# A three-layer float32 block on one core: the depthwise conv's VectorE sums kept in PSUM, its steps spread wider, and SBUF pools padded to multiples of 512 bytes

## The chip, the cores and the metric

One core of a Trainium2 chip. The time is microseconds (us) of device time of one launch; the profile is one execution of the same program. TensorE multiplies out of SBUF into PSUM (8 banks of 512 float32 per partition), VectorE, ScalarE and GpSimd work on SBUF, VectorE and ScalarE on PSUM too, and SyncE issues the DMAs.

## What is computed

Three layers over 512 tokens of width 1024, all float32. The first layer is differential attention, a gated FFN with a width-3 conv, and a gated embedding; the second has windowed attention in place of the first. The third, which the change touches, mixes a conv branch and an attention branch, and ends in an FFN without a conv:

```python
proj = h @ w_in                      # 1024 conv columns, q, k, v, forget, two gates of 1024
a = a_in[..., :512] * sigmoid(a_in[..., 512:])
a = causal_depthwise_conv(a, w_dw, b_dw)          # 512 channels, 31 taps
y_conv = silu(layernorm(a, g_ln, b_ln)) @ w_conv_out
y_attn = forgetting_attention(q, k, v, f) @ w_attn_out
merged = sigmoid(gate_a) * y_conv + sigmoid(gate_b) * y_attn
x = x + merged @ w_out
x = x + (silu(g) * u) @ w_ffn_out    # g, u = rmsnorm(x) @ w_ffn_in
```

## The kernel before

Activations lie with channels on the partitions and the 512 tokens along the free axis. A float32 product is made of three float32r ones: each operand is split into a high part and a rest, and `mm3` (L185) issues high*high (L187), high*rest (L188) and rest*high (L189). Weights come in units of 128x1024 by a DMA on SyncE's queue, ScalarE casts the high part `wh` (L156), VectorE subtracts for the rest `wl` (L157); two raw and three split units are in flight. `dense` (L292) makes one 128x512 output of 24 matmuls. The stationary operand is the weight, the moving one the activation: `xO`, `xV` and `xq` from the pool `xp`, `gh` and `gl` (the FFN's hidden tiles) from the pool `gp`, `mg` (half of the merged branch in the third layer) from a pool `mg`.

In `mix` (L857) the third layer's first half is built. The depthwise conv is done off TensorE: four chunks of 128 channels, 31 taps each. `glu` and `glu_gate` leave a chunk's input in `pads[m]` and `accs[m]` takes the sum. Chunks 2 and 3, and the last 11 taps of chunk 1, belong to GpSimd: a product into a scratch tile (`tap`, three buffers) on GpSimd itself during the attention heads (L915) or on ScalarE afterwards (L917), and an add on GpSimd (L918). All 31 taps of chunk 0 and the first 20 of chunk 1 are VectorE's: L909 for the first tap of a chunk, then `scalar_tensor_tensor` with the sum read and written in place (L911). `keep` holds the order of these as written. During the eight heads a few GpSimd taps follow each step (`TAPS`). Then come 16 gates (`gate`, L1074: one `dense` each, evacuated by L1076 into `tb` or `ga`, then Tanh), 8 products of the attention branch (`attn_conv(tb[m], 1, ox)`, 12 matmuls each, moving operand `xq`), 8 of the conv branch (`attn_conv(t, 0, cx)`, moving operands `cxh` and `cxl`), and `w_out2`.

`conv_step(i)` is called after gate i. For the first `CSTEP` gates it issues an even share of the taps that are left, afterwards one step of `conv_norm` (L1095), the layer norm over the four chunks: sum over chunks (L1090 to L1092), split, two matmuls against ones (`ps_cs`), centring (L1104) and squares, sum, mean by matmul (L226), inverse root, a broadcast matmul (`ps_bc`), scaling (L1116), SiLU and split into `cx`.

The order on an engine is not the order of the code alone: a list scheduler at build time takes what is ready on its own estimated timeline, earlier code first. A matmul output takes the next PSUM bank of a cycle (`WIDE`, six banks; outside wide stretches two): `acc` has two, `sc` three, `po` one; `tp`, two more, is for transposes and small sums. In the wide stretch of the gates the heads' `po` bank is part of the cycle.

SBUF is laid out pool after pool, each tile rounded up to 32 bytes, the first one (`sp`) at 128 bytes past a multiple of 512. Added up so, every large tile of the pools `hp`, `wp`, `xp` and `fp` (`h`, `wr`, `wh`, `wl`, `xq`, `xO`, `xV`, scratch) starts 32 bytes past a multiple of 512, and those of the pools opened after `sm` (`gh`, `gl`, `mg`, `rt`, `kst`, `tb`) start 192 bytes past one. A weight block inside a unit is 512 bytes wide, so it keeps its unit's offset.

Of the kernel before, what the change touches and what calls it, by code (L numbers as in the profile page):

```python
# [11 lines left out]
F32 = mybir.dt.float32  # L12
F32R = mybir.dt.float32r
I32 = mybir.dt.int32
AF = mybir.ActivationFunctionType
ALU = mybir.AluOpType
# [3 lines left out]
P = 128  # L20
D = 1024
T = 512
KD = D // P
# [24 lines left out]

VT = (31, 20)
TAPS = ((0, 1),) * 5 + ((0, 2),) * 3  # L50
CSTEP = 7

BANKS = {"acc": 2, "sc": 3, "po": 1}
WIDE = ("acc", "sc", "acc", "sc", "sc", "po")
# [5 lines left out]
_SPW = 0  # L60
# [24 lines left out]
_CNW = 641  # L85
# [6 lines left out]
def build(tc, nc, a, out):  # L92
    c = Ctx()
    es = ExitStack()
    cp = es.enter_context(tc.tile_pool(name="cp", bufs=1))
# [4 lines left out]
    sm = es.enter_context(tc.tile_pool(name="sm", bufs=4))  # L100
    dr = es.enter_context(tc.tile_pool(name="dr", bufs=1, space=bass.MemoryType.DRAM))
    acc = es.enter_context(tc.tile_pool(name="acc", bufs=2, space=PSUM))
    att = es.enter_context(tc.tile_pool(name="att", bufs=2, space=PSUM))

    V, S, G, TE, Q = nc.vector, nc.scalar, nc.gpsimd, nc.tensor, nc.sync


    sp = cp.tile([P, _SPW], F32, name="sp")
    cn = cp.tile([P, 641], F32, name="cn")
    onesf = cp.tile([P, P], F32, name="onesf")  # L110
    onesr = cp.tile([P, P], F32R, name="onesr")
    epsc = cp.tile([P, 1], F32, name="epsc")
    Q.dma_start(out=sp[:, 0:KD], in_=a["sp"][:, 0:KD])
    V.memset(onesf, 1.0)
    V.memset(epsc, EPS)
# [6 lines left out]
    def spc(name, i=0, n=1):  # L122
        o, w = _SP[name]
        return sp[:, o + i : o + i + n]

    def rd(t):
        return t.bitcast(F32)
# [49 lines left out]
    def split(hi, lo, src, scale=None):  # L177
        if scale is None:
            S.copy(out=hi, in_=src)
            V.tensor_tensor(out=lo, in0=src, in1=rd(hi), op=ALU.subtract)  # L180
        else:
            S.activation(out=hi, in_=src, func=AF.Copy, scale=scale)
            V.scalar_tensor_tensor(out=lo, in0=src, scalar=scale, in1=rd(hi), op0=ALU.mult, op1=ALU.subtract)  # L183
# [19 lines left out]
    def row_mm(ps, rt, eng, stop):  # L203

        r2 = sm.tile([P, 2, 4], F32R, tag="r2", name="r2")
        V.tensor_copy(r2[:, 0], rt)
        V.tensor_tensor(out=r2[:, 1], in0=rt, in1=rd(r2[:, 0]), op=ALU.subtract)
        for z in range(2):
            dg = fp.tile([P, 4, P], F32R, tag="C", name="dg")
            eng.tensor_tensor(  # L210
                out=dg,
                in0=ident[:, None, :].to_broadcast([P, 4, P]),
                in1=rd(r2[:, z])[:, :, None].to_broadcast([P, 4, P]),
                op=ALU.mult,
            )
            TE.matmul(ps, onesr, dg.rearrange("p a b -> p (a b)"), start=z == 0, stop=z == 1 and stop)
# [6 lines left out]
    def token_mean(ss, dst, scale, eps=EPS):  # L223
        ps = att.tile([P, 4], F32, tag="tp", name="ps_tm")
        for t in range(4):
            TE.matmul(ps[:, t : t + 1], ss[:, t * P : (t + 1) * P], onesf[:, 0:1], start=True, stop=True)  # L226
        V.tensor_scalar(out=dst, in0=ps, scalar1=scale, scalar2=eps, op0=ALU.mult, op1=ALU.add)
# [52 lines left out]
    tags = {"next": cycle(("acc",))}  # L280

    def wide(on):

        tags["next"] = cycle(WIDE if on else ("acc",))

    def bank(shape=(P, T)):
        t = next(tags["next"])
        return (acc if t == "acc" else att).tile(list(shape), F32, tag=t, name="ps_d", bufs=BANKS[t])
# [139 lines left out]
    def diff_attention(nm, nxt):  # L428
        x = nm.x
        pes = ExitStack()  # L430
        ap = pes.enter_context(tc.tile_pool(name="ap0", bufs=2, reuse_waits="tile"))
        lam = sm.tile([P, 1], F32, tag="lam", name="lam", bufs=1)
        lt = sm.tile([P, 2, 64], F32, tag="lt", name="lt", bufs=1)
        lv = spc("lam", 0, 256).rearrange("p (a b d) -> p a b d", a=2, b=2)
        V.tensor_tensor(out=lt, in0=lv[:, :, 0], in1=lv[:, :, 1], op=ALU.mult)
# [421 lines left out]
    def mix(nm, nxt):  # L857
# [4 lines left out]
        ma = aes.enter_context(tc.tile_pool(name="ma", bufs=1, reuse_waits="tile"))  # L862
        trir = ma.tile([P, P], F32R, name="trir")
        idr = ma.tile([P, P], F32R, name="idr")
        nid = ma.tile([P, 8], F32R, name="nid")
        blkr = ma.tile([P, P], F32R, name="blkr")
        V.tensor_copy(trir, tri)
        V.tensor_copy(idr, ident)
# [11 lines left out]
        NT = 31  # L880
        pads, accs = {}, {}
# [21 lines left out]
        keep = tc.keep_in_program_order  # L903

        def tap(m, j, eng, alone):
            src = pads[m][:, j : j + T]
            w = dwh[:, m * NT + j : m * NT + j + 1]
            if j == 0:
                V.tensor_scalar(out=accs[m], in0=src, scalar1=w, scalar2=spc("bdw", m), op0=ALU.mult, op1=ALU.add)  # L909
            elif eng is V:  # L910
                keep(V.scalar_tensor_tensor(out=accs[m], in0=src, scalar=w, in1=accs[m], op0=ALU.mult, op1=ALU.add))  # L911
            else:
                t = fp.tile([P, T], F32, tag="C", name="tap")
                if alone:
                    keep(G.tensor_tensor(out=t, in0=src, in1=w.to_broadcast([P, T]), op=ALU.mult))  # L915
                else:
                    keep(S.activation(out=t, in_=src, func=AF.Copy, scale=w))  # L917
                G.tensor_tensor(out=accs[m], in0=accs[m], in1=t, op=ALU.add)  # L918

        bgv, bgp = deque(), deque()  # L920

        def taps(nv, np_, alone=False):
            for q, n in ((bgv, nv), (bgp, np_)):
                for _ in range(min(n, len(q))):
                    tap(*q.popleft(), alone)
# [11 lines left out]
        fq, y, z, w = (sm.tile([P, 32], F32, tag="f" + n, name="f" + n, bufs=1) for n in "qyzw")  # L937
# [128 lines left out]
                    next(gens[fl.popleft()], None)  # L1066
            late = g
        next(late)
        wide(True)
        aes.close()  # L1070
        ges = ExitStack()
        gp = ges.enter_context(tc.tile_pool(name="mg", bufs=1, reuse_waits="tile"))
# [8 lines left out]
        def attn_conv(t, j, src):  # L1081

            ps = bank()
            wca[j].mm(ps, [src[k] for k in range(4)])
            V.scalar_tensor_tensor(out=t, in0=t, scalar=1.0, in1=ps, op0=ALU.add, op1=ALU.mult)


        def chan_sum(tiles):
            s = [fp.tile([P, T], F32, tag="A", name="cs") for _ in range(2)]
            G.tensor_tensor(out=s[0], in0=tiles[2], in1=tiles[3], op=ALU.add)  # L1090
            V.tensor_tensor(out=s[1], in0=tiles[0], in1=tiles[1], op=ALU.add)
            V.tensor_tensor(out=s[1], in0=s[1], in1=s[0], op=ALU.add)  # L1092
            return s[1]

        def conv_norm():  # L1095
            s = chan_sum(accs)
            sh, sl = (fp.tile([P, T], F32R, tag="C", name="csh") for _ in range(2))
            split(sh, sl, s)
            ps = att.tile([P, T], F32, tag="tp", name="ps_cs")
            TE.matmul(ps, onesr, sh, start=True, stop=False)  # L1100
            TE.matmul(ps, onesr, sl, start=False, stop=True)
            sqs = {}
            for m in (2, 3, 0, 1):
                V.scalar_tensor_tensor(out=accs[m], in0=ps, scalar=-1.0 / 512, in1=accs[m], op0=ALU.mult, op1=ALU.add)  # L1104
                sqs[m] = fp.tile([P, T], F32, tag="B", name="csq", bufs=4)
                S.activation(out=sqs[m], in_=accs[m], func=AF.Square)
            yield
            s = chan_sum(sqs)
            v = sm.tile([P, 4], F32, tag="nv", name="nv")
            token_mean(s, v, 1.0 / 512)  # L1110
            ps = att.tile([P, T], F32, tag="tp", name="ps_bc")
            row_mm(ps, rsqrt_small(v, 4), V, True)
            yield
            cx = [mp.tile([P, T], F32R, tag="cv", name="cxh", bufs=8) for _ in range(4)]
            for m in range(4):
                V.tensor_tensor(out=accs[m], in0=accs[m], in1=ps, op=ALU.mult)  # L1116
                t = fp.tile([P, T], F32, tag="B", name="csi", bufs=4)
                act(out=t, in_=accs[m], func=AF.Silu, scale=spc("lng", m), bias=spc("lnb", m))
                lo = mp.tile([P, T], F32R, tag="cv", name="cxl", bufs=8)
                split(cx[m], lo, t)  # L1120
                cx[m] = (cx[m], lo)
            yield cx


        cn_ = conv_norm()
        for m in (1, 0):
            glu_gate(m)
        tb, ga, cx = [], [], None

        def conv_step(i):  # L1130
            if i < CSTEP:
                n = CSTEP - i
                taps(-(-len(bgv) // n), -(-len(bgp) // n))
                return None
            return next(cn_, None)

        for m in range(2 * KD):
# [6 lines left out]
                ga.append(gq[:, m % 4])  # L1144
                gate(ga[-1], 0, m - KD)
            cx = conv_step(m) or cx
        for _ in range(3):
            cx = conv_step(2 * KD) or cx
        for m in range(KD):
            attn_conv(tb[m], 1, ox)  # L1150
        mq = Quads()
        mx = []
        for m in range(KD):
# [16 lines left out]
    for k in range(KD):  # L1170
# [1 line left out]
        if k == 1:  # L1172
            early["w_qk0", 2] = wunit("w_qk0", 2, 1024)
        n0.add(k)
    Q.dma_start(out=cn, in_=a["cn"])
    Q.dma_start(out=sp[:, KD:], in_=a["sp"][:, KD:])
    for i in (3, 0):
        early["w_qk0", i] = wunit("w_qk0", i, 1024)
    rope_tables()
# [143 lines left out]
```

## Time and profile before

| what | value |
|---|---|
| median of 3 runs | 2132.37 us (2131.36 to 2133.54) |
| the profiled execution's own time | 2130.8 us |
| its span, first to last instruction | 2129.0 us |
| mean granted TensorE clock | 0.982 of full speed |
| busy share: TensorE, VectorE, ScalarE, GpSimd | 95%, 66%, 42%, 22% |

A span is read from an engine's rows in order of time; "idle before" is what an engine waited just ahead of an instruction, and the arrow names what released it. Matmuls overlap, so a matmul's listed duration is longer than the distance from its start to the next one's start; the distance is what counts for time, and is worked out here from first and last starts.

### The profile page before, as it was taken

To read this page: it belongs to the slowest core of one execution; us is meant where nothing else is said; L and a number is where in the kernel's file an instruction comes from. 1 tells how busy PE (TensorE), PEld (TensorE's weight loads), DVE (VectorE), ACT (ScalarE), POOL (GpSimd) and SP (SyncE) were. 2 spreads that over 40 slices of the span, in tenths; PEclk is the share of its full clock that TensorE was granted. 3 is DMA by queue.
4 is the path that set the end of the run, shared out by engine and by line. 5 is a ranking of instruction groups with operands and counts; after the bars stand their busy time and mean duration, and the time that the engine had idled before them with its cause. 6 is when DMAs were issued, how large, how long until landed. Compare 5 with 4: busy or idle time off the path is not lost.

```text
span 2129.0 us, 25047 instructions
## 1 busy us (share of the span) xinstructions
PE 2027.6 (95%) x9374; PEld 1656.7 (78%) x9374; DVE 1402.7 (66%) x2188; ACT 900.1 (42%) x1431; POOL 460.6 (22%) x323
## 2 busy tenths in 40 slices
PE   7999989999999998989999999999897799999999
PEld 6788768888888876768888888788776588888887
DVE  7777868557376757777557476879889765434343
ACT  5565644334244535554334244555544343223221
POOL 2464330000002246220000002305795230000000
PEclk9999989999999999999999999999999999999999
DMA  4634312222223263112222223233312122222222
GB/s 165 171 111 126 130 60 99 99 98 91 99 99 129 99 173 95 42 48 99 96 93 99 97 93 138 71 110 104 97 57 70 69 99 90 99 100 95 93 99 89
DMA packets 69465, 212.43 MB, mean 100 GB/s; under 512 B 9568, under 2 KB 9568, under 8 KB 68832
## 3 DMA queue, kind: packets, MB, share of 16 engines
q1 hardware_dynamic: 69344, 210.84, 30.2%
q8 instruction: 74, 1.21, 0.2%
q14 instruction: 47, 0.39, 0.1%
HBM read 179.31 MB, written 6.29 MB: 87 GB/s over the span
## 4 chain that ended last, share of the span: by engine, by line
PE 79%; DVE 12%; ACT 2%; issue 2%; DMA 2%; SPq 1%; POOL 1%; DVEq 0%; ACTq 0%; POOLq 0%
PE ps_d L187 25%; PE ps_d L189 24%; PE ps_d L188 24%; DVE cacc L911 3%; DVE wl L157 2%; PE ps_s L394 1%; PE ps_o L188 1%; PE ps_o L187 1%; PE ps_o L189 1%; PE ps_s L395 1%; SPq L384 1%; DVE e L1021 1%; ACT e L145 1%; DVE e L648 1%; DMA qst<-rt 1%
## 5 line engine op out<-in xcount | busy, mean ns | idle before, releaser
L156 ACT CAST wh<-wr 128x1024 fp32r<-128x1024 f32 (+1 forms) x323 | 337.8, 1048 | 678.4 <-PE ps_d L188 558.8
L189 PE MATMUL ps_d<-xO,wl 128*128 128x512 f32 (+1 forms) x1400 | 549.5, 393 | 12.0 <-DVE wl L157 12.0
L187 PE MATMUL ps_d<-xO,wh 128*128 128x512 f32 x1400 | 549.7, 393 | 7.2 <-ACT wh L156 4.8
L188 PE MATMUL ps_d<-xV,wh 128*128 128x512 f32 (+1 forms) x1400 | 548.8, 392 | 0.0
L157 DVE TENSOR_TENSOR wl<-wr,wh 128x1024 fp32r<-128x1024 f32 x286 | 364.3, 1275 | 86.3 <-ACT wh L156 83.9
L189 PEld LDWEIGHTS ps_d<-xO,wl 128*128 128x128 f32 (+1 forms) x1400 | 264.1, 189 | 70.1 <-DVE wl L157 13.9
L187 PEld LDWEIGHTS ps_d<-xO,wh 128*128 128x128 f32 x1400 | 264.3, 189 | 64.4 <-ACT wh L156 6.1
L188 PEld LDWEIGHTS ps_d<-xV,wh 128*128 128x128 f32 (+1 forms) x1400 | 264.4, 189 | 56.5 <-DVE xV L183 0.2
L270 POOL TENSOR_TENSOR ss<-ss,sq 128x512 f32<-128x512 f32 x44 | 69.4, 1577 | 822.9 <-ACT sq L268 810.3
L313 DVE TENSOR_TENSOR u<-ps_d,rb 128x512 f32<-128x512 f32 x156 | 106.3, 687 | 204.4 <-PE ps_d L189 197.2
L188 PE MATMUL ps_d<-gl,wh 128*128 128x512 f32 x528 | 208.2, 396 | 0.0
L187 PE MATMUL ps_d<-gh,wh 128*128 128x512 f32 x528 | 206.9, 396 | 0.0
L189 PE MATMUL ps_d<-gh,wl 128*128 128x512 f32 x528 | 206.8, 396 | 0.0
L187 PE MATMUL ps_d<-xq,wh 128*128 128x512 f32 x448 | 178.4, 402 | 20.4 <-ACT wh L156 8.7
L189 PE MATMUL ps_d<-xq,wl 128*128 128x512 f32 x448 | 178.6, 399 | 3.4 <-DVE wl L157 3.3
L188 PE MATMUL ps_d<-xq,wh 128*128 128x512 f32 x448 | 178.6, 399 | 1.0 <-DVE xq L183 1.0
L762 DVE TENSOR_TENSOR h<-h,ps_d 128x512 f32<-128x512 f32 x72 | 48.6, 686 | 189.3 <-PE ps_d L189 189.3
L189 PEld LDWEIGHTS ps_d<-gh,wl 128*128 128x128 f32 x528 | 99.5, 188 | 24.3
L188 PEld LDWEIGHTS ps_d<-gl,wh 128*128 128x128 f32 x528 | 99.5, 188 | 24.2
L187 PEld LDWEIGHTS ps_d<-gh,wh 128*128 128x128 f32 x528 | 99.4, 188 | 24.1
L187 PEld LDWEIGHTS ps_d<-xq,wh 128*128 128x128 f32 x448 | 86.2, 193 | 40.4 <-ACT wh L156 8.9
L157 POOL TENSOR_TENSOR wl<-wr,wh 128x1024 fp32r<-128x1024 f32 x37 | 90.5, 2449 | 110.1 <-ACT wh L156 76.7
(309 smaller groups left out, 3138.9 us busy)
## 6 DMA issues: line engine op xcount, KB each, us to landing
wr<-w_up SPq DMA_DIRECT2D x132, 512.0 KB, 3.5
wr<-w_dn SPq DMA_DIRECT2D x66, 512.0 KB, 3.5
wr<-w_qk SPq DMA_DIRECT2D x34, 512.0 KB, 3.6
qst<-rt SPq DMA_DIRECT2D x64, 128.0 KB, 2.7
wr<-w_pg SPq DMA_DIRECT2D x16, 512.0 KB, 3.5
wr<-w_g SPq DMA_DIRECT2D x16, 512.0 KB, 3.5
wr<-w_v SPq DMA_DIRECT2D x14, 512.0 KB, 3.5
st<-qhl SPq DMA_DIRECT2D x48, 128.0 KB, 2.3
```

The lines of the kernel that those rows point to most:

```text
L145: i = S.activation(**kw)
L156: S.copy(out=hi, in_=raw)
L157: lo_eng[0].tensor_tensor(out=lo, in0=raw, in1=rd(hi), op=ALU.subtract)
L187: TE.matmul(ps, lh, rh, start=start, stop=False)
L188: TE.matmul(ps, lh, rl, start=False, stop=False)
L189: TE.matmul(ps, ll, rh, start=False, stop=stop)
L270: (V if self.first and k not in SSP else G).tensor_tensor(out=self.ss, in0=self.ss, in1=sq, op=ALU.add)
L313: V.tensor_tensor(out=u, in0=ps, in1=rb, op=ALU.mult)
L384: Q.dma_start(out=rd(t[64 * b : 64 * b + 64]), in_=rd(hl[32 * j : 32 * j + 32, 2 * z : 2 * z + 2]))
L394: TE.matmul(ps, q[:, qc], k[:, kc], start=True, stop=False)
L762: V.tensor_tensor(out=h[m], in0=h[m], in1=ps, op=ALU.add)
L911: keep(V.scalar_tensor_tensor(out=accs[m], in0=src, scalar=w, in1=accs[m], op0=ALU.mult, op1=ALU.add))
```

## The change

It does four things. VectorE's conv sums of chunks 0 and 1 go into two PSUM banks (`pacc`, the `po` bank and one of `tp`); the last tap of chunk 0 writes `accs[0]` in SBUF; chunk 1's GpSimd part starts with ScalarE's product written straight into `accs[1]`, and a VectorE add in `conv_norm` brings the two parts together. `CSTEP` goes from 7 to 12, and `conv_norm` has six steps in place of three, of which the last may follow products of the attention branch. The gates and the attention branch's products cycle over five banks (without `po`); the six return after them. Tiles of the pools `cp`, `sm` and `ma` are widened. Added up as above, all large tiles of `hp`, `wp`, `xp`, `fp` and of the pools opened after `sm` then start at a multiple of 512 bytes (in `mix`, the conv's own `cv` tiles of 2176 bytes at multiples of 128, and the head tiles 64 past a multiple).

```diff
-CSTEP = 7
+CSTEP = 12
...
-    sp = cp.tile([P, _SPW], F32, name="sp")
-    cn = cp.tile([P, 641], F32, name="cn")
+    sp = cp.tile([P, 896], F32, name="sp")
+    cn = cp.tile([P, 704], F32, name="cn")
...
-    epsc = cp.tile([P, 1], F32, name="epsc")
+    epsc = cp.tile([P, 16], F32, name="epsc")[:, 0:1]
...
-        lam = sm.tile([P, 1], F32, tag="lam", name="lam", bufs=1)
+        lam = sm.tile([P, 96], F32, tag="lam", name="lam", bufs=1)[:, 0:1]
...
-        nid = ma.tile([P, 8], F32R, name="nid")
+        nid = ma.tile([P, 16], F32R, name="nid")[:, 0:8]
...
             if j == 0:
-                V.tensor_scalar(out=accs[m], in0=src, scalar1=w, scalar2=spc("bdw", m), op0=ALU.mult, op1=ALU.add)
+                if eng is V:
+                    pacc[m] = att.tile([P, T], F32, tag=("po", "tp")[m], name="pacc", bufs=(BANKS["po"], 2)[m])
+                V.tensor_scalar(out=pacc.get(m, accs[m]), in0=src, scalar1=w, scalar2=spc("bdw", m), op0=ALU.mult, op1=ALU.add)
             elif eng is V:
-                keep(V.scalar_tensor_tensor(out=accs[m], in0=src, scalar=w, in1=accs[m], op0=ALU.mult, op1=ALU.add))
+                out = accs[m] if j == NT - 1 else pacc[m]
+                keep(V.scalar_tensor_tensor(out=out, in0=src, scalar=w, in1=pacc[m], op0=ALU.mult, op1=ALU.add))
+            elif m < 2 and j == VT[m]:
+                keep(S.activation(out=accs[m], in_=src, func=AF.Copy, scale=w))
...
-        wide(True)
+        tags["next"] = cycle(WIDE[:5])
         aes.close()
...
         def conv_norm():
+            for m in range(2):
+                if VT[m] < NT:
+                    V.tensor_tensor(out=accs[m], in0=pacc[m], in1=accs[m], op=ALU.add)
             s = chan_sum(accs)
             sh, sl = (fp.tile([P, T], F32R, tag="C", name="csh") for _ in range(2))
             split(sh, sl, s)
+            yield
...
             s = chan_sum(sqs)
+            yield
             v = sm.tile([P, 4], F32, tag="nv", name="nv")
             token_mean(s, v, 1.0 / 512)
+            yield
...
-        for _ in range(3):
-            cx = conv_step(2 * KD) or cx
         for m in range(KD):
             attn_conv(tb[m], 1, ox)
+            cx = conv_step(2 * KD) or cx
+        wide(True)
...
-    Q.dma_start(out=cn, in_=a["cn"])
-    Q.dma_start(out=sp[:, KD:], in_=a["sp"][:, KD:])
+    Q.dma_start(out=cn[:, 0:_CNW], in_=a["cn"])
+    Q.dma_start(out=sp[:, KD:_SPW], in_=a["sp"][:, KD:])
```

## Rows read from the trace of the kernel before

**Rows 1.** The page: the chain by line, and three costly groups.
```profile
PE ps_d L187 25%; PE ps_d L189 24%; PE ps_d L188 24%; DVE cacc L911 3%; DVE wl L157 2%; PE ps_s L394 1%; PE ps_o L188 1%; PE ps_o L187 1%; PE ps_o L189 1%; PE ps_s L395 1%; SPq L384 1%; DVE e L1021 1%; ACT e L145 1%; DVE e L648 1%; DMA qst<-rt 1%
...
L187 PE MATMUL ps_d<-xO,wh 128*128 128x512 f32 x1400 | 549.7, 393 | 7.2 <-ACT wh L156 4.8
...
L187 PE MATMUL ps_d<-gh,wh 128*128 128x512 f32 x528 | 206.9, 396 | 0.0
L187 PE MATMUL ps_d<-xq,wh 128*128 128x512 f32 x448 | 178.4, 402 | 20.4 <-ACT wh L156 8.7
```

**Rows 2.** Busy by stretch: us, PE, PEld, DVE, ACT, POOL, PEclk, DMA share, GB/s.
```profile
450.00:530.00 80.00, 80.00 (x354) 66.25 (x353) 56.63 (x72) 35.52 (x44) 0.00 (x0) 1.00 0.29 99
536.00:576.00 40.00, 40.00 (x172) 32.18 (x171) 16.30 (x19) 7.89 (x8) 0.00 (x0) 1.00 0.27 92
...
1575.00:1692.00 117.00, 92.62 (x377) 73.82 (x375) 112.60 (x122) 51.31 (x72) 62.25 (x40) 0.92 0.19 67
```

**Rows 3.** Waits, 1570 to 1700 us: who for whom, total us, times, longest.
```profile
PE ps_d L189 <- DVE wl L157: 13.7, 4, 6.9
...
PE ps_cs L1100 <- ACT csh L179: 6.3, 1, 6.3
...
PE ps_d L187 <- ACT cxh L179: 4.4, 1, 4.4
...
PEld ps_d L187 <- DVE tb L1076: 0.3, 1, 0.3
```

**Rows 4.** Groups, 1575 to 1700 us: count, busy us, mean ns, idle before.
```profile
L911 DVE SCALAR_TENSOR_TENSOR cacc<-pad,dwh,cacc 128x512 f32<-128x512 f32 x49 | 61.2, 1288 | 0.2
...
L188 PE MATMUL ps_d<-xV,wh 128*128 128x512 f32 x88 | 35.6, 404 | 0.0
L157 DVE TENSOR_TENSOR wl<-wr,wh 128x1024 fp32r<-128x1024 f32 x15 | 22.0, 1465 | 0.6 <-ACT wh L156 0.6
...
L188 PE MATMUL ps_d<-xq,wh 128*128 128x512 f32 x32 | 13.1, 409 | 0.0
...
L909 DVE TENSOR_SCALAR cacc<-pad,dwh,sp 128x512 f32<-128x512 f32 x2 | 2.7, 1384 | 0.0
...
L1104 DVE SCALAR_TENSOR_TENSOR cacc<-ps_cs,cacc 128x512 f32<-128x512 f32 x4 | 2.5, 682 | 0.0
```

**Rows 5.** Timelines of DVE and of POOL: start us, length us, merged instructions.
```profile
1611.03 6.88 DVE L911 SCALAR_TENSOR_TENSOR cacc<-pad,dwh,cacc 128x512 f32<-128x512 f32 x4
...
1629.41 2.73 DVE L911 SCALAR_TENSOR_TENSOR cacc<-pad,dwh,cacc 128x512 f32<-128x512 f32 x4
...
1663.14 1.21 DVE L157 TENSOR_TENSOR wl<-wr,wh 128x1024 fp32r<-128x1024 f32 x1
...
1610.89 6.46 POOL L918 TENSOR_TENSOR cacc<-cacc,tap 128x512 f32<-128x512 f32 x4 [0.87 <-ACT tap L917]
...
1641.71 19.70 POOL L918 TENSOR_TENSOR cacc<-cacc,tap 128x512 f32<-128x512 f32 x11 [15.17 <-DVE cacc L911]
```

**Rows 6.** The tile tb: min/median/max ns, first and last start us.
```profile
L1076 DVE TENSOR_TENSOR tb<-ps_d,rb x8: 673/678/680, 1575.1 to 1608.8; 128x512 f32<-128x512 f32 x8
```

**Rows 7.** Tiles gh, xV in an FFN: min/median/max ns, first, last start.
```profile
L187 PE MATMUL ps_d<-gh,wh x64: 392/397/400, 534.1 to 578.4; 128*128 128x512 f32 x64
...
L188 PE MATMUL ps_d<-xV,wh x128: 389/389/393, 447.3 to 533.6; 128*128 128x512 f32 x128
```

**Rows 8.** Groups on PE, 1722 to 1762 us (w_out2): mg and xq move.
```profile
L188 PE MATMUL ps_d<-mg,wh 128*128 128x512 f32 x30 | 11.7, 397 | 0.0
...
L188 PE MATMUL ps_d<-xq,wh 128*128 128x512 f32 x26 | 10.1, 390 | 0.0
```

**Rows 9.** Timeline: the stage's first gate matmul, VectorE's last tap, the first conv product.
```profile
1575.83 0.75 PE L187 MATMUL ps_d<-xO,wh 128*128 128x512 f32 x1
...
1664.28 0.74 DVE L911 SCALAR_TENSOR_TENSOR cacc<-pad,dwh,cacc 128x512 f32<-128x512 f32 x1
...
1692.24 0.63 PE L187 MATMUL ps_d<-cxh,wh 128*128 128x512 f32 x1 [4.39 <-ACT cxh L179]
```

More of the change, by code (lines that the diff above doesn't have):

```diff
@@ L918, in tap @@
                 G.tensor_tensor(out=accs[m], in0=accs[m], in1=t, op=ALU.add)
-        bgv, bgp = deque(), deque()
+        bgv, bgp, pacc = deque(), deque(), {}
         def taps(nv, np_, alone=False):
```

## The prediction, made before any run of the change

> **What bounds the kernel now.** I read the page first. The chain that ended last is mostly the three dense matmul lines, so over most of the span only a faster matmul stream would count; the one large foreign item among them is VectorE's conv sum, `cacc` L911, at 3% [rows 1]. So there are two questions: what the stage of that line loses, and how fast matmuls follow each other elsewhere.
>
> For the first I took the stretch 1575 to 1692 us, from the first gate matmul behind the attention heads to the first conv product [rows 9]. In its 117 us VectorE is busy 112.6 and TensorE 92.6, with the granted clock at 0.92, the idle time included [rows 2]. VectorE is the bound here. The waits say how: TensorE waits 13.7 us in four places for `wl`, the low part of the next weights, which is queued on VectorE behind taps; then 6.3 us for the layer norm's split and 4.4 us for `cx` [rows 3]. The stretch holds 88 + 32 triples, 360 matmuls of 512 columns [rows 4]. At the undisturbed distance of 226.7 ns (below) they need 81.6 us, against 116.4 from 1575.8 to 1692.2. So 34.8 us are lost, the most that any repair of this stage can return.
>
> Why VectorE is slow there is seen in two timelines. While GpSimd runs its adds, four taps take 6.88 us, 1.72 each; in a gap of GpSimd, four take 2.73, 0.68 each [rows 5]. Each tap reads two SBUF tensors (`pad` and `cacc`). Evacuations of gates, which read one PSUM and one SBUF tensor, take 673 to 680 ns throughout, in the stretches with GpSimd too [rows 6]. So it is the second SBUF input that pays. GpSimd pays as well, 1.62 us an add [rows 5].
>
> For the second question: in an FFN chunk 64 matmuls L187 on `gh` start from 534.1 to 578.4 us, every third of the stream, so 44.3/63/3 = 234.4 ns apart; 128 on `xV` go from 447.3 to 533.6, 226.5 to 226.7 [rows 7]. Both stretches have TensorE fully busy at clock 1.00 [rows 2]. In `w_out2` the two sorts alternate inside one output and carry halves of the same activation: `mg` lists 397 ns, `xq` 390 [rows 8], as `gh` and `xV` do. What `gh` and `mg` share is their place: 192 bytes past a multiple of 512, with weights at 32; `xO`, `xV` and `xq` have the weights' own offset. I read this as a clash between the moving stream and the loading of the next weights, spared where both have the same offset. That is an inference: no row shows an offset changed alone.
>
> **The change part by part.** I sum against the profiled execution, 2130.8 us, 1.6 below the median.
>
> *Taps in PSUM.* 51 instructions lose their second SBUF input: 49 L911 with 61.2 us and the first taps L909 with 2.7 [rows 4]. No VectorE instruction in this profile's stage writes PSUM, so I bound: 0.62 us (four L1104, which read a PSUM tensor, end to end in 2.5) from below [rows 4], 1.72 from above if nothing is relieved [rows 5]. Nearest are the forms with one PSUM input and the undisturbed tap; I take 0.67, 34.2 us in all, a saving of 29.7.
> [...]
>
> *When the last tap ends.* VectorE starts the stage at 1575.1 with five evacuations (3.1), one split (0.7) and two conv inputs (2.4), as before, to 1581.3. Then 51 taps (34.2), ten evacuations (6.8) and ten `wl`. These keep two SBUF inputs, so they stay exposed to GpSimd: 1.465 mean, 1.21 undisturbed [rows 4, 5]. With GpSimd busy 53% of the time [rows 2] a fully exposed one is about 1.21 + 0.255/0.53 = 1.69. I take 14.7 us (12.1 to 16.9). The last tap ends near 1637.0, against 1665.0 now [rows 9]. GpSimd has 28 adds left; at 1.62 us that is 45, done by about 1631, and its adds of chunk 1 no longer wait 15.2 us for VectorE's sum in the same tile [rows 5].
>
> *To the conv products.* From the last tap to the first conv product it is 27.2 us now [rows 9], VectorE's layer norm between evacuations of the attention branch. The new add of chunk 1 costs 0.7 and is ready early. So the first product comes at about 1664.9; TensorE's own work would allow 1575.8 + 81.6 = 1657.4. The gain is 27 us. Its ends: 34.8 at TensorE's floor, and 15 if taps cost 0.75, all `wl` are fully exposed and the norm is 6 us longer.
>
> *Twelve gates, finer steps, five banks.* Five gates are computed before 1575, so their share of the taps was 36 of 51 that ranked ahead of the next `wl`, and becomes 21. That moves waits, not VectorE's sum; norm steps rank later but are ready only after the last tap, so they stand where their data stands. On ScalarE the extra product for `accs[1]` replaces one L917; SyncE's loads are the same bytes, and no DMA is issued by a moved step. What is queued behind the new add is the first chunk sum, which needs it anyway. The bank given up costs nothing while five gates (27 us of matmuls) may wait for evacuation; the only bank wait now is 0.3 us [rows 3]. All this at 0; its ends, 6.3 us either way (the wait at `ps_cs`), lie within those above.
>
> *Padding.* 1584 matmuls on `gh` and `gl` (three groups of 528) [rows 1] would go from 234.4 to 226.7 ns: 12.2 us, all in stretches where TensorE never waits [rows 2]. 96 on `mg` add 0.7; `cx` keeps mixed offsets. I take 12.7, between 0 and 13.5. The other engines and the DMAs I leave at 0; no row bears on them.
>
> Sum: 27 + 12.7 = 39.7, so 2091.1 for the profiled execution and **2093 us** for the median.
>
> **The rivals.**
> *Padding buys nothing*: `gh` is slow for another reason. For it: no row separates place from tile. Then 2106 us (2097 to 2117).
> [...]
> *The taps are not relieved*, because a PSUM sum updated in place is as slow as the disturbed tap. Against it stand the forms with a PSUM input [rows 4, 6]. Then only the padding counts: 2120 us.
> *Slower: offset 0 is worse than 32.* If not the equal offset but 32 itself spares the clash, the 5544 matmuls on `xO`, `xV` and `xq` (three groups of 1400 and of 448) [rows 1] go to 234.4: +42.7, and `gh` stays. With the stage's 27 that is 2132.4 - 27 + 42.7 = 2148 us. It decides from 27/5544 = 4.9 ns on. For it, `gh` at 192 is slow, so being off 32 is what all slow ones share too; against it, a rule that favours 32 alone is odder than one of equal offsets.
> [...]
>
> **How the numbers follow.** Forecast 0.69 (its own range 2084 to 2105), padding nothing 0.15, taps not relieved 0.05, much faster 0.06, slower 0.04, and 0.01 for no change; a run of this kernel can tell 0.2%, some 4 us, from none. The range 2083 to 2114 holds the forecast and most of the second case, and leaves the others out. Faster 0.95, same 0.01, slower 0.04.
>
> **What would show it.** Right: L911 with one mean near 0.7 us while GpSimd adds; the first conv product some 90 us after the first gate matmul instead of 116; TensorE's waits for `wl` mostly gone; `gh` matmuls listed at 389 ns and 226.7 apart, `xV` unchanged. Wrong: L911 in two lengths again; conv products late with VectorE still full, or waiting for GpSimd's last add; `gh` at 397; `xV` at 397, which is the slower case.

## The result, and the profile after the change

The changed kernel takes 2097.57 us (median; 2094.45 to 2098.10), the kernel before 2132.44 beside it: a ratio of 0.983, interval 0.982 to 0.985, so 34.9 us faster. The forecast was 2093 in a range of 2083 to 2114. The profiled execution of the changed kernel took 2097.09 us with a span of 2095.3; against 2130.8 before, 33.7 us to account for.

Behind the edit lines have moved on by one to some ten numbers: `mm3` is L188 to L190, `wl` L158, VectorE's first taps L912, the others L915, GpSimd's adds L924, gate evacuations L1083, the new add L1105. The page, its chain and four groups, answers to [rows 1]:

```profile
PE 80%; DVE 9%; POOL 5%; issue 2%; ACT 2%; DMA 2%; SPq 1%; DVEq 0%; POOLq 0%; ACTq 0%
PE ps_d L188 25%; PE ps_d L190 24%; PE ps_d L189 24%; POOL cacc L924 3%; POOL tap L921 1%; DVE wl L158 1%; PE ps_o L189 1%; PE ps_s L395 1%; PE ps_o L188 1%; PE ps_o L190 1%; PE ps_s L396 1%; DMA qst<-rt 1%; SPq L385 1%; PE ps_t L674 1%; DVE xq L184 1%
...
L188 PE MATMUL ps_d<-xO,wh 128*128 128x512 f32 x1400 | 547.2, 392 | 5.6 <-ACT wh L157 3.2
...
L189 PE MATMUL ps_d<-gl,wh 128*128 128x512 f32 x528 | 204.3, 389 | 0.0
L188 PE MATMUL ps_d<-gh,wh 128*128 128x512 f32 x528 | 203.0, 389 | 0.0
L190 PE MATMUL ps_d<-gh,wl 128*128 128x512 f32 x528 | 203.0, 389 | 0.0
```

VectorE's conv sum is no longer among the items of the chain that the page lists; GpSimd's sum stands in its place, with the same 3%. That is a question for the experiments: is GpSimd the new bound? The down products list 389 ns like those on `xO`, no longer 396.

The conv stage by stretch of the changed kernel (us, then busy time and instructions of PE, PEld, DVE, ACT, POOL, granted clock, DMA share, GB/s): up to VectorE's last tap, from there to the first conv product, and the whole.

```profile
1567.50:1637.00 69.50, 68.40 (x299) 55.50 (x297) 65.86 (x82) 41.44 (x59) 55.09 (x38) 0.99 0.23 76
1637.00:1663.30 26.30, 19.33 (x79) 15.16 (x79) 21.97 (x43) 9.83 (x14) 1.30 (x1) 0.89 0.32 100
1567.50:1663.30 95.80, 87.73 (x378) 70.66 (x376) 87.83 (x124) 51.26 (x73) 56.39 (x39) 0.96 0.26 82
```

The stage has shrunk from 117.0 to 95.8 us [rows 2]. VectorE and TensorE are now equally full in it, and GpSimd, with about the same number of adds, is busy 55.1 of the 69.5 us to the last tap. The groups of that stretch on VectorE, and its taps with least, median and greatest length, answer to [rows 4, 5]:

```profile
L915 DVE SCALAR_TENSOR_TENSOR pacc<-pad,dwh,pacc 128x512 f32<-128x512 f32 x48 | 33.7, 743 | 0.1
L158 DVE TENSOR_TENSOR wl<-wr,wh 128x1024 fp32r<-128x1024 f32 x10 | 18.4, 1842 | 2.9 <-ACT wh L157 2.9
...
L912 DVE TENSOR_SCALAR pacc<-pad,dwh,sp 128x512 f32<-128x512 f32 x2 | 1.5, 800 | 0.0
```
```profile
L915 DVE SCALAR_TENSOR_TENSOR pacc<-pad,dwh,pacc x48: 736/742/756, 1575.1 to 1634.8; 128x512 f32<-128x512 f32 x48
L915 DVE SCALAR_TENSOR_TENSOR cacc<-pad,dwh,pacc x1: 748/748/748, 1635.6 to 1635.6; 128x512 f32<-128x512 f32 x1
```

One length for all taps, 0.74 us, whatever GpSimd does; but `wl` has become dearer: the ten up to the last tap take 1.84 us each, where the ten ahead of the last tap of before took 15.9 us in all, 1.59 each. And VectorE waits 2.9 us for `wh` ahead of them, where it waited for none before. The waits of the stage, which answer to [rows 3] (who for whom, total us, times, longest):

```profile
ACT tap L923 <- POOL cacc L924: 16.7, 17, 1.9
...
PE ps_d L188 <- ACT cxh L180: 3.4, 1, 3.4
...
DVE wl L158 <- ACT wh L157: 3.1, 7, 1.0
...
PE ps_cs L1111 <- ACT csh L180: 2.8, 1, 2.8
...
DVE cacc L1105 <- POOL cacc L924: 0.5, 1, 0.5
...
PE ps_d L190 <- DVE wl L158: 0.2, 1, 0.2
```

TensorE's 13.7 us for `wl` are down to 0.2. The first row has grown: before it was 10.8 us in 11 waits, the longest 1.7. ScalarE's tap products wait for GpSimd to free their buffers, and what stands behind them on ScalarE, the `wh` of the gates among it, comes late to VectorE.

The stage's ends and a down chunk in the trace of the changed kernel answer to [rows 9, 7]:

```profile
1568.28 0.69 PE L188 MATMUL ps_d<-xO,wh 128*128 128x512 f32 x1
...
1635.62 0.75 DVE L915 SCALAR_TENSOR_TENSOR cacc<-pad,dwh,pacc 128x512 f32<-128x512 f32 x1
...
1663.27 2.08 PE L188 MATMUL ps_d<-cxh,wh 128*128 128x512 f32 x4 [3.35 <-ACT cxh L180]
```
```profile
L188 PE MATMUL ps_d<-gh,wh x61: 389/389/390, 404.6 to 445.4; 128*128 128x512 f32 x61
...
L189 PE MATMUL ps_d<-xV,wh x128: 389/389/390, 447.7 to 534.1; 128*128 128x512 f32 x128
```

From first gate matmul to first conv product it is 95.0 us, 21.4 less than the 116.4 of before. The down products are (445.4 - 404.6)/60/3 = 226.7 ns apart, the up products 86.4/127/3 = 226.8, as before. On 1584 matmuls the first is worth 12.0 us (4.0 in each layer between the first and last starts of its down chunks), and `mg`, now listed at 389 ns, brings 0.83 in `w_out2`, from its first to its last matmul. Stage and padding make 34.2. The 0.5 us that this is above the measured 33.7 is what the other stages leave: 1.9 us lost ahead of the first down product, 0.4 in the second layer up to its down products, and 1.8 won between the second layer's FFN and the conv stage; no run here explains these.

### The profile page after: what moved, and what is told of

Same layout as the page of the kernel before. It is cut to its first block, busy times and chain, and to the rows that moved or that the text cites. A ratio compares the mean times of both kernels' runs of the same rounds, so it can differ in the third digit from the quotient of the medians.

```text
span 2095.3 us, 25046 instructions
## 1 busy us (share of the span) xinstructions
PE 2013.4 (96%) x9374; PEld 1655.5 (79%) x9374; DVE 1378.0 (66%) x2189; ACT 899.4 (43%) x1431; POOL 454.7 (22%) x322
## 4 chain that ended last, share of the span: by engine, by line
PE 80%; DVE 9%; POOL 5%; issue 2%; ACT 2%; DMA 2%; SPq 1%; DVEq 0%; POOLq 0%; ACTq 0%
PE ps_d L188 25%; PE ps_d L190 24%; PE ps_d L189 24%; POOL cacc L924 3%; POOL tap L921 1%; DVE wl L158 1%; PE ps_o L189 1%; PE ps_s L395 1%; PE ps_o L188 1%; PE ps_o L190 1%; PE ps_s L396 1%; DMA qst<-rt 1%; SPq L385 1%; PE ps_t L674 1%; DVE xq L184 1%
## 5 line engine op out<-in xcount | busy, mean ns | idle before, releaser
L188 PE MATMUL ps_d<-xO,wh 128*128 128x512 f32 x1400 | 547.2, 392 | 5.6 <-ACT wh L157 3.2
L190 PE MATMUL ps_d<-xO,wl 128*128 128x512 f32 (+1 forms) x1400 | 547.2, 391 | 0.8 <-DVE wl L158 0.8
L158 DVE TENSOR_TENSOR wl<-wr,wh 128x1024 fp32r<-128x1024 f32 x286 | 367.3, 1286 | 90.3 <-ACT wh L157 87.9
L188 PEld LDWEIGHTS ps_d<-xO,wh 128*128 128x128 f32 x1400 | 262.8, 188 | 62.5 <-ACT wh L157 4.5
L190 PEld LDWEIGHTS ps_d<-xO,wl 128*128 128x128 f32 (+1 forms) x1400 | 262.7, 188 | 57.5 <-DVE wl L158 2.0
L271 POOL TENSOR_TENSOR ss<-ss,sq 128x512 f32<-128x512 f32 x44 | 69.4, 1577 | 815.4 <-ACT sq L269 801.9
L188 PE MATMUL ps_d<-gh,wh 128*128 128x512 f32 x528 | 203.0, 389 | 0.0
L190 PE MATMUL ps_d<-gh,wl 128*128 128x512 f32 x528 | 203.0, 389 | 0.0
L188 PE MATMUL ps_d<-xq,wh 128*128 128x512 f32 x448 | 179.3, 404 | 21.8 <-ACT wh L157 10.1
L190 PE MATMUL ps_d<-xq,wl 128*128 128x512 f32 x448 | 179.4, 401 | 1.3 <-DVE wl L158 1.3
L188 PEld LDWEIGHTS ps_d<-xq,wh 128*128 128x128 f32 x448 | 86.7, 194 | 41.9 <-ACT wh L157 10.3
L188 PEld LDWEIGHTS ps_d<-gh,wh 128*128 128x128 f32 x528 | 99.1, 188 | 20.6
L190 PEld LDWEIGHTS ps_d<-gh,wl 128*128 128x128 f32 x528 | 99.1, 188 | 20.6
L158 POOL TENSOR_TENSOR wl<-wr,wh 128x1024 fp32r<-128x1024 f32 x37 | 90.5, 2449 | 109.0 <-ACT wh L157 94.3
```

The lines of the kernel that those rows point to most:

```text
L158: lo_eng[0].tensor_tensor(out=lo, in0=raw, in1=rd(hi), op=ALU.subtract)
L188: TE.matmul(ps, lh, rh, start=start, stop=False)
L190: TE.matmul(ps, ll, rh, start=False, stop=stop)
L271: (V if self.first and k not in SSP else G).tensor_tensor(out=self.ss, in0=self.ss, in1=sq, op=ALU.add)
```

## Experiments

From here on the conv stage is counted from the first gate evacuation to the first conv product: 117.1 us in the kernel before and 95.7 in the changed one.

**Each part alone.** The padding without the conv, and the conv without the padding, against the kernel before and the changed kernel:

```diff
 padding alone, against before (cn, epsc, lam, nid likewise)
-    sp = cp.tile([P, _SPW], F32, name="sp")
+    sp = cp.tile([P, 896], F32, name="sp")
...
 conv alone, against the changed kernel
-    sp = cp.tile([P, 896], F32, name="sp")
+    sp = cp.tile([P, _SPW], F32, name="sp")
...
```

> The kernel before with the padding alone. Theory (a matmul is slow when its moving operand and the next weights lie at different offsets modulo 512 bytes; padding makes them equal for gh, gl and mg): the 1584 matmuls on gh and gl go from 234.3 to 226.7 ns apart, 12.0 us in the traces of before and after, and mg gives 0.7, so 2119 to 2121 us, with the conv stage (first gate evacuation to first conv product) left at 117 us. Rival (padding does nothing, the gain of the down products comes along with something else in the change): 2131 to 2134 us.

> The changed kernel without the padding: PSUM sums, twelve gates and finer steps alone. Theory (the two parts lie in different stretches and add up): the stage is 95 to 97 us instead of 117.2, the gh and gl matmuls stay listed at 397 ns, and the time is 2132.4 - 21.4 = 2111, within 2108 to 2113. Rival (the stage gained because matmuls of gates or of mg became faster through the offsets): the stage loses clearly less than 21 us without the padding, and the time is above 2115.

Padding alone: 2116.3 us against 2131.7 beside it, 15.3 less, with the interval of the ratio (0.991 to 0.994) from 12.4 to 18.8; its stage is 117.2 us. Conv alone: 2110.6, 21.1 less (17.7 to 23.9); its stage is 96.4 us, and its `gh` matmuls list 397 ns. The two parts lie apart and add up. Padding alone came out 3 us below the range expected; the interval covers the 12.8 us that the down products and `mg` explain. In that kernel only the places of tiles differ, and the down products go from 397 to 389 ns:

```profile
L187 PE MATMUL ps_d<-gh,wh x528: 389/389/389, 402.3 to 2109.8; 128*128 128x512 f32 x176
```

**PSUM sums without the new order, and the new order without PSUM.** Both against the changed kernel:

```diff
 PSUM sums, old order (the added yields go out as well)
-CSTEP = 12
+CSTEP = 7
...
 new order, sums in SBUF (pacc, its ScalarE line and the added L1105 go out)
-                out = accs[m] if j == NT - 1 else pacc[m]
-                keep(V.scalar_tensor_tensor(out=out, in0=src, scalar=w, in1=pacc[m], op0=ALU.mult, op1=ALU.add))
+                keep(V.scalar_tensor_tensor(out=accs[m], in0=src, scalar=w, in1=accs[m], op0=ALU.mult, op1=ALU.add))
...
```

> The changed kernel with its taps spread over seven gates again and the norm in its three old steps; PSUM sums, five gate banks and padding stay. Theory (the taps' price is what counts, 51 taps at about 0.74 us instead of up to 1.72; where they stand among the gates moves little, because VectorE is the bound in either order): 2093 to 2102 us. Rival (the spreading is what frees TensorE, since seven gates crowd VectorE and the gates then wait for their banks): at least half of the stage's 21.4 us is lost, 2107 us or more.

> The changed kernel with VectorE's sums back in SBUF; twelve gates, finer steps, five banks and padding stay. Theory (the taps' price counts): taps beside GpSimd's adds cost about 1.7 us again, two lengths in the trace, the stage is 112 to 120 us, and the time is 2115 to 2122 us, that of the padding alone or a few us better. Rival (the spreading makes the gain): taps fit between the gates at either price, the stage stays below 103 us, and the time is 2097 to 2104 us.

PSUM in the old order: 2099.6 us, 0.985 (0.983 to 0.987), not told apart from the changed kernel, with a stage of 95.4 us. The new order with sums in SBUF: 2117.4, 0.993 (0.992 to 0.995), the padding's gain and no more, with a stage of 116.9. VectorE's groups in the two stages:

```profile
L915 DVE SCALAR_TENSOR_TENSOR pacc<-pad,dwh,pacc 128x512 f32<-128x512 f32 x48 | 33.8, 745 | 0.1
L158 DVE TENSOR_TENSOR wl<-wr,wh 128x1024 fp32r<-128x1024 f32 x15 | 24.0, 1598 | 2.7 <-ACT wh L157 2.7
```
```profile
L912 DVE SCALAR_TENSOR_TENSOR cacc<-pad,dwh,cacc 128x512 f32<-128x512 f32 x49 | 60.3, 1267 | 0.2
L158 DVE TENSOR_TENSOR wl<-wr,wh 128x1024 fp32r<-128x1024 f32 x15 | 22.6, 1505 | 0.6 <-ACT wh L157 0.6
```

So the sums in PSUM make all of the stage's gain, and twelve gates with finer steps none that can be seen. The same edit frees GpSimd's adds from waiting 15.2 us for VectorE's sum of chunk 1 [rows 5]; that was not tried by itself, but the 49 taps alone differ by more than the gain, 60.3 us against 34.5 with the one that writes SBUF.

**GpSimd taken away.** The same line in the kernel before and in the changed kernel; both then leave out 29 of the conv's taps:

```diff
-            for q, n in ((bgv, nv), (bgp, np_)):
+            for q, n in ((bgv, nv), (bgp, np_ if alone else 0)):
```

> The kernel before without GpSimd's taps behind the attention heads (29 of the depthwise conv's 124 taps, those of ScalarE and GpSimd, are left out there; the rest is as before). Theory (taps are slow because VectorE and GpSimd read SBUF at the same time): all 49 taps on L911 at about 0.68 us, none above 1 us, VectorE no longer full, and the stage from 117 to about 90 us. Rival (the taps are slow for a reason of their own, such as adding in place in SBUF behind a write): a mean well above 1 us stays although GpSimd is idle.

> The changed kernel without GpSimd's taps behind the attention heads (the same 29 of 124 taps are left out). Theory (what the forecast missed in the stage, 68.8 us instead of 61.9 to the last tap, is the rest of the contention with GpSimd in the wl of the gates, and ScalarE's gate activations queued behind tap products that wait for GpSimd to free their buffers): wl back at 1.2 us instead of 1.63, no wait of VectorE for wh, the last tap 5 to 8 us earlier, the first conv product with it or bounded by TensorE's own 82 us, and taps unchanged at 0.74. Rival (taps in PSUM cost more than 0.68 because of GpSimd): taps at 0.67 to 0.68, and the waits for wh remain.

Both were timed once, without an interval. Before without these taps: 2104.1 us, its stage 89.2 us instead of 117.1. Its taps, still summed in SBUF:

```profile
L911 DVE SCALAR_TENSOR_TENSOR cacc<-pad,dwh,cacc x49: 731/736/1774, 1585.0 to 1637.6; 128x512 f32<-128x512 f32 x49
```

The few long ones are the first, while GpSimd finishes taps begun in the heads (its last instruction starts at 1587.7); from then on all list 0.73 to 0.75. The edit takes ScalarE's products for these taps away too, but the kernel before tells the two apart: of its 49 taps the 20 that meet no instruction of GpSimd all list 0.73 to 0.74 us, and of the four from 1629.41 on [rows 5] the first three run beside ScalarE's products and a cast:

```profile
1628.26 1.93 ACT L917 ACTIVATE tap<-pad,dwh 128x512 f32<-128x512 f32 x3
1630.10 1.04 ACT L156 CAST wh<-wr 128x1024 fp32r<-128x1024 f32 x1
```

So the clash is with GpSimd, as the theory says, and the undisturbed SBUF tap is as long as the PSUM tap, 0.736 us against 0.742 (medians). The two hold each other up: in the kernel before a tap lists up to 1.79 us beside GpSimd and 0.74 without it, and an add of GpSimd 1.62 us beside such taps [rows 5], but 1.29 to 1.30 beside the changed kernel's taps in PSUM, in the 14 adds from 1577 us on that meet no `wl`.

The changed kernel without them: 2093.9 us, 3.7 below its median, stage 91.3. In the taps' part of it, VectorE's `wl` and taps:

```profile
L158 DVE TENSOR_TENSOR wl<-wr,wh x10: 1215/1216/1806, 1578.5 to 1625.2; 128x1024 fp32r<-128x1024 f32 x10
```
```profile
L915 DVE SCALAR_TENSOR_TENSOR pacc<-pad,dwh,pacc x48: 741/747/756, 1576.0 to 1627.2; 128x512 f32<-128x512 f32 x48
```

The taps have not changed (0.747 us against 0.742), so GpSimd costs them nothing any more. `wl` has a median of 1.22 us, the waits for `wh` are down from 3.1 to 0.4 us, and the last tap ends 60.3 us into the stage instead of 68.8, 8.5 earlier. The first conv product comes only 4.5 earlier: the tail behind the last tap is 31.0 us instead of 26.9, since VectorE now waits in it 6.9 us for TensorE instead of 3.4. GpSimd's sum is the largest item beside the matmuls in the chain of the changed kernel, but its 29 taps, with ScalarE's products for them, are worth 4.5 us.

**What is left in the stage.** Buffers of their own for the tap products; with these, VectorE's taps split evenly (24 and 24 instead of 31 and 20, three fewer in all); and four fewer again:

```diff
-                t = fp.tile([P, T], F32, tag="C", name="tap")
+                t = fp.tile([P, T], F32, tag="C", name="tap") if alone else gp.tile([P, T], F32, tag="tap", name="tap", bufs=4)
 even split (24, 24), or (22, 22), as well
-VT = (31, 20)
+VT = (24, 24)
```

> The changed kernel with tap products behind the heads in four buffers of their own, and nothing else. Theory (3.1 us of VectorE's time before the last tap is waiting for wh, because ScalarE's tap products wait 16.7 us for GpSimd to free their buffers and hold up the activations behind them): these waits fall below 1 us, the last tap comes 2 to 3 us earlier, 2094 to 2096 us. Rival (ScalarE is held by GpSimd's pace, not by the number of buffers): waits for wh stay near 3 us, and the time at 2096 to 2099.

> The changed kernel with VectorE's taps split 24 and 24 over chunks 1 and 0 (it was 20 and 31, so that 11 taps of chunk 0 stood alone at the end, each waiting for the one before: 0.78 us apart against 0.66), and with tap products behind the heads in four buffers of their own. Theory (the forecast's missing us in the stage are chained taps and ScalarE's queue behind GpSimd's tap buffers): all taps 0.66 us apart, 48 instead of 51, no waits of VectorE for wh, the last tap 62 to 64 us after the stage's start instead of 68.8, the first conv product 3 to 5 us earlier, 2092 to 2095 us. Rival (TensorE's queue or GpSimd sets the first conv product by now): the last tap comes earlier, but the product does not, and the time stays within 2 us of the changed kernel's 2097.6.

> As the balanced split, but 22 and 22, four taps more for GpSimd. Theory: VectorE is done earlier still, and GpSimd, whose last add was 57.4 us into the stage, takes 7 more adds of some 1.7 us and ends at about 69 us, so that GpSimd is the bound: the first chunk sum waits for it, and the time is within 2 us of the changed kernel's, 2096 to 2099. Rival (GpSimd's adds become faster with VectorE's second input in PSUM and buffers of their own): the time falls below that of the 24 and 24 split.

Own buffers: 2095.9 us, 0.982 (0.981 to 0.984). Waits on VectorE in its stage:

```profile
DVE cacc L1105 <- POOL cacc L924: 1.9, 1, 1.9
DVE wl L158 <- ACT wh L157: 1.8, 6, 0.4
```

The waits for `wh` fall from 3.1 to 1.8, but the new add now waits 1.9 us for GpSimd's last add to chunk 1 instead of 0.5, and the last tap comes only 0.7 us earlier, not 2 to 3. ScalarE's products still wait 15.1 us for GpSimd (16.7 before this edit), so most of what holds ScalarE is GpSimd's pace; neither theory had it whole.

Even split: 2094.9 us, 0.982 (0.981 to 0.983). The last tap ends at 64.5 us, 4.3 earlier, a little later than expected; `wh` is still waited for (3.0 us), and the product comes 1.9 us earlier, not 3 to 5. With 22 and 22: 2095.6 us (0.982, 0.981 to 0.983; 2096 to 2099 expected), the last tap at 59.0, but GpSimd's last add at 65.2, and VectorE waits for it:

```profile
DVE cacc L1105 <- POOL cacc L924: 3.3, 1, 3.3
```

The first product is again at 93.8 us, as with the even split. All three lie 1.7 to 2.7 us below the changed kernel, whose interval overlaps each of theirs; none is shown to be faster. In the even split TensorE is busy 87.1 of the stage's 93.8 us (columns as above):

```profile
1566.68:1660.51 93.83, 87.06 (x377) 70.38 (x378) 87.07 (x122) 53.00 (x76) 59.58 (x41) 0.98 0.25 84
```

TensorE is idle in 6.8 us of it. From the first gate matmul this stage takes 93.1 us, 11.5 above the 81.6 that the prediction gives for TensorE's work alone. So some 7 to 11 us are still open here; no run wins them.

**Which places clash.** The changed kernel with the down products' operands moved to six other places, a pair per layer (for this `gh` and `gl` get buffers of their own), and then with the weights moved instead:

```diff
 a small tile ahead of gh and one ahead of gl, of other size in each layer
+        o1, o2 = {0: (8, 8), 1: (24, 8), None: (64, 32)}[conv]
+        V.memset(gp.tile([P, o1], F32, name="rul1", bufs=1), 0.0)
...
+                    V.memset(gp.tile([P, o2], F32, name="rul2", bufs=1), 0.0)
...
 weights moved (a small tile ahead of x keeps x at 0)
-    sp = cp.tile([P, 896], F32, name="sp")
+    sp = cp.tile([P, 888], F32, name="sp")
```

> The changed kernel with gh and gl at six other places: modulo 512 bytes, gh and gl lie at 32 and 64 in the first layer, 96 and 128 in the second, 256 and 384 in the third, against weights at 0. Theory (any difference of offsets modulo 512 costs the same): in all three layers the down products go from 226.7 to about 234 ns apart and from 389 to 397 ns listed, 12 us in all, some 2109 us. Rival (only some differences clash, for instance those modulo 64 or 128 bytes): matmuls of one layer or of gl alone stay at 389 ns, and the time is less by 2 us for each tile kind of a layer that is spared; with 64, 128, 256 and 384 spared it is some 2101 us.

> The changed kernel with the matmuls' weights (and the residual h) shifted to 480 modulo 512 bytes, while all moving operands stay at 0. Theory (it is the difference between moving operand and weights that counts): all 7200 matmuls on xO, xV, xq, gh, gl and mg go from 226.7 to about 234 ns apart, 7.6 x 7200 = 55 us where TensorE is the bound, some 2150 us (2135 to 2160). Rival (the moving operand's own place counts, 0 modulo 512 being good by itself): gaps stay at 226.7 ns and the time within 2095 to 2100 us.

Both were timed once. Six places: 2107.4 us, 9.8 above the changed kernel. The groups of the first, second and third layer:

```profile
L189 PE MATMUL ps_d<-gl,wh 128*128 128x512 f32 x176 | 68.8, 394 | 0.0
...
L188 PE MATMUL ps_d<-gh,wh 128*128 128x512 f32 x176 | 68.2, 394 | 0.0
...
L189 PE MATMUL ps_d<-gl,wh 128*128 128x512 f32 x176 | 68.6, 393 | 0.0
L188 PE MATMUL ps_d<-gh,wh 128*128 128x512 f32 x176 | 68.6, 396 | 0.0
...
L189 PE MATMUL ps_d<-gl,wh 128*128 128x512 f32 x176 | 69.3, 395 | 0.0
L188 PE MATMUL ps_d<-gh,wh 128*128 128x512 f32 x176 | 68.6, 391 | 0.0
L190 PE MATMUL ps_d<-gh,wl 128*128 128x512 f32 x176 | 68.3, 389 | 0.0
```

At 32, 64, 96 and 128 bytes from the weights the tiles are slow, 393 to 396 ns listed; so is `gl` at 384, with 395. `gh` at 256 is mostly fast: a median of 389 ns listed. But in the third layer's last chunk, from 2077 us to the end, it is slow as well. The two parts of that chunk, from the groups of 2069 to 2077 and of 2078 to 2100 us:

```profile
L188 PE MATMUL ps_d<-gh,wh 128*128 128x512 f32 x12 | 4.5, 389 | 0.0
```
```profile
L188 PE MATMUL ps_d<-gh,wh 128*128 128x512 f32 x32 | 12.7, 397 | 0.0
```

So the theory fell in one point, and the rival in three of the four places it would spare. A difference of 256 bytes can be free, but is not reliably so; what ended it at 2077 us is open. Equal offsets gave 226.7 in every down chunk of the changed kernel.

Weights moved: 2133.6 us, 36 above the changed kernel, and all the dense matmuls are slow (394 to 396 ns listed, the medians of the groups on high*rest), though no moving operand was touched (the residual `h` moved along with the weights). A down and an up chunk of it:

```profile
L189 PE MATMUL ps_d<-gh,wh x64: 393/395/397, 407.6 to 451.7; 128*128 128x512 f32 x64
...
L190 PE MATMUL ps_d<-xV,wh x128: 393/395/397, 452.6 to 541.5; 128*128 128x512 f32 x128
```

Both are 233.3 ns apart (44.1/63/3 and 88.9/127/3). Weights and operands both at 32 were fast before [rows 7], both at 0 are fast now, and moving either alone is slow, 233.3 ns here and 393 to 396 listed for most of the operands above: it is the difference that costs. The time expected, 2150 (2135 to 2160), was too high: it charged 7200 matmuls with 7.6 ns. From first up to last down product the three layers' FFNs take 1112.4 us instead of 1081.2, which is 6.6 ns on the 4752 matmuls in them. The other 2448 would be 16 us at this price, and the rest of the profiled execution lost 5.3; that other engines set the pace there for much of the time is a reading, not tested.

## Why the prediction was right

The measured 2097.6 lies in the forecast's own range (2084 to 2105), but just as well at the near end of the range of *padding buys nothing* (2097 to 2117). The time alone does not tell the two apart; the padding alone does, and so do the distances of the down products.

*The stage's bound and its loss* hold. VectorE was the bound through taps that read two SBUF tensors beside GpSimd: without GpSimd the same kernel's stage falls by 28 us. Of the 34.8 us lost, 21.4 came back.

*Taps in PSUM at 0.67, 34.2 us in all* was right. They list 0.74, but start 0.66 apart where chunks alternate (four in 2.72 us at 1585.77) and 0.79 where one chunk stands alone (three in 2.33 at 1629.42); from each start to the next the 51 take 34.8 us of VectorE's time. A running sum in PSUM lists much the same as one in SBUF that nothing disturbs: 0.742 us against 0.736, and 0.748 for the one tap that reads PSUM and writes SBUF.

*The last tap at 61.9 us, the gain of 27* is the step that was mis-sized: 68.8 and 21.4. Its failing term is the ten `wl`, priced 14.7 us (12.1 to 16.9) and measured at 18.4. I had taken the mean of 1.465 us from fifteen of them, of which five stand behind the last tap, where GpSimd has a single instruction left; the ten that were priced took 15.9 before. The share of 53% for GpSimd was that of the whole stage too: up to the last tap it was 60.9/89.9 = 68% before, and in the shorter stretch it is 55.1/69.5 = 79%. An exposed `wl` costs up to 2.1 us, not 1.69, and the trace of before had three of 2.3 us in the stage, two of them:

```profile
1590.41 2.31 DVE L157 TENSOR_TENSOR wl<-wr,wh 128x1024 fp32r<-128x1024 f32 x1
...
1652.89 2.29 DVE L157 TENSOR_TENSOR wl<-wr,wh 128x1024 fp32r<-128x1024 f32 x1
```

The second miss is the 2.9 us that VectorE waits for `wh`; I had ScalarE at no cost and named nobody who waits behind its tap products. The third is the new add: it was put outside, but stands ahead of the last tap with 0.7 us and 0.5 of waiting. Counted from each start to the next (listed lengths run some 0.08 us into the next instruction), the 6.9 us that are missing are `wl` 2.95, `wh` 2.86, the add 1.12, the taps 0.60 and small gaps 0.15, less 0.75 for evacuations that are shorter than I took them. The run without GpSimd bears out the first two: both go, and the last tap is at 60.3.

*From the last tap to the product* 27.9 us were forecast, 0.7 of them for the add, which came earlier, and 26.9 measured. *Twelve gates, finer steps, five banks at 0*: right for the order, by the run without it; the banks alone were not tried.

*Padding 12.7* was right (12.0 + 0.83), and so was the inference that unequal offsets cost time, now shown by moving either side alone. That it is the loading of the next weights that clashes with the moving stream is still an inference: the runs show distances, not where they arise.

*The rivals.* Padding nothing: the padding alone refutes it, and so do the matmuls that go from 226.7 to 233.3 ns apart with only the weights and `h` moved. Taps not relieved: one length for all. Offset 0 worse, or much faster: `xV` is 226.8 ns apart at 0, and was 226.5 to 226.7 at 32.

*What would show it* came true in each sign but one: the first product some 90 us after the first gate matmul, where 95.0 was measured.

## What to carry to other kernels

When VectorE and GpSimd work side by side, keep one input of VectorE's running sums in PSUM (here 0.74 us a tap whatever GpSimd did, instead of up to 1.79), and price what keeps two SBUF inputs by what an exposed one costs, and by GpSimd's share in the shortened stretch, not by a mean over the old stage. For matmuls like these, lay out SBUF so that moving operands and weights have the same offset modulo 512 bytes (here 226.7 ns apart, against 233.3 and 234.4 at 32 and 160 bytes from each other); one small tile ahead of them shifts everything behind it. A chain that names a new engine tells where to look; what that engine is worth is told by taking its work away.

## What was not expected of the hardware

The distance between matmuls depends on the difference of two SBUF addresses modulo 512 bytes: for these dense matmuls it is 226.7 to 226.8 ns at 0, 233.3 at 32 (weights moved) and 234.4 at 160 (the kernel before). The listed lengths go the same way: 389 ns at 0, 393 to 396 at 32, 64, 96, 128 and 384, and at 256 either 389 or 397 in one and the same kernel. An instruction that adds to the sum of the one just before starts 0.78 to 0.79 us after it, one that adds to another sum 0.66, in PSUM (above) as in SBUF (three taps of one chunk in 2.31 us in the kernel before without GpSimd, four that alternate in 2.73 [rows 5]). And cutting GpSimd's 29 taps from either kernel leaves stages of 89.2 and 91.3 us, so as far as two single runs tell, PSUM has no worth of its own here beyond the relief from GpSimd.
